# An encoder layer on one core: raw tiles of two gate/up jobs in query slots, a row norm behind a product, the last products in program order, and w_down raws on GpSimd's queue

## The chip, the cores and the metric

The kernel runs on one core of one Trainium2 chip. The metric is the device time of one execution in microseconds (us); lower is better. The times of before are the median of three runs and their extremes. One further execution was recorded by the hardware profiler, and every row below is of that one. Engines are named as in the profile: PE (TensorE's matmuls), DVE (VectorE), ACT (ScalarE), POOL (GpSimd), SP (SyncE, which here only issues DMAs).

## What is computed

One layer of a bidirectional encoder over two sequences of 512 tokens, width 1024, all in float32:

```
u = rms_norm(h, ln1);  z = u @ w_in            # pool_in 512 | c_q 384 | c_kv 256 | k_rope 32
y_pool = (window means of pool_in - pool_in) @ w_pool * pool_scale
q  = rms_norm(c_q)  @ w_qb;  k, v = rms_norm(c_kv) @ w_kvb   # 8 heads, rope, norms of q and k
h += concat(y_pool, softmax(q k^T) v) @ w_o
u2 = rms_norm(h, ln2);  h += (silu(u2 @ w_gate) * (u2 @ w_up)) @ w_down   # w_gate, w_up 1024 x 2816
out = h + sigmoid(rms_norm(h, ple_norm) @ w_ple_gate) * (p @ w_ple_proj)
```

## The kernel before

Activations lie with features on the 128 partitions and the 512 tokens of a sequence along the row, so a matmul writes a 128x512 PSUM bank. Every operand is held as a high and a low part, and one product of two 128-blocks is three matmuls (`mm3`, lines L157, L158, L159: high·high, then the two mixed ones). ACT makes the high part (L130), DVE or POOL the low part by a subtraction (`split`, L132 and L133).

The order of each engine's instructions is made by a scheduler from the program as it is written, and each engine then works its list strictly in order. Tiles come from tags with a fixed number of slots; a new tile of a tag waits until the readers of the tile that held its slot are done. So an edit to a tag or to the program's order moves rows on several engines.

The stages, in order of time. `latents()` (5 to 77 us) multiplies x by w_cq and w_ckv (`product`), and between them makes the row norm of x: `norm_columns` sums squares and takes the root on POOL, `norm_rows` makes `diag` on DVE (L203), multiplies it with ones on PE (L205, tile `rb`) and copies the result out on ACT (L209). `latent_norm` then squares c_q and c_kv on ACT (L330, tile `junk`). Pooling, projections and attention follow, then `output` (w_o).

The gate, up, down and gated-embedding products are Strassen-like. For a pair of weight blocks, `seven` runs seven products of n·3 matmuls each, named by the activation piece they take: B11, B21, T1, T2, T4, T3, B22. The activation pieces are sums and differences of normed halves: `normed_first` makes tiles x0 of sequence 0 (tag QK, 8 slots; the B21 pieces lie in the other four), `normed_rest` the norms of sequence 1 (L734) and the differences for T1 (L633), T2 (L763) and T4 (L766, the last readers of x0). The T4 pieces take the slots of x0 afterwards. The weight combinations are made by a generator, `stationary`: it loads two raw blocks (`load`, L143) and yields seven operand tiles from sums s (L648) and splits w (L130, L133). Operands are made up to eight ahead of the products (`fill`), in the order of the list `jobs`.

The first four gate/up jobs are cut in two: their part 0 gives only B11 and B21, part 1 the other five, so that part 1 loads the raws once more (tag R, 2 slots, on SP's queue). The hidden pieces made from gate and up are written to DRAM (`spill`, on SP's queue, tiles `st`, tensors op...) and read back by POOL's queue (`loaded`, tiles u, 512 KB each) for the w_down products; the saved h comes back the same way (`h_again`). w_down is worked in groups of (2, 3, 3, 3) blocks of rows; the 8 raw tiles of its first group (128x512, 256 KB) lie in tag F. The kernel ends with the gated embedding: `finish` applies the sigmoid, multiplies by the embedding (L986), adds h (L987) and stores.

Of the kernel before, what the change touches and what calls it, by code (L numbers as in the profile page):

```python
# [1 line left out]

# [1 line left out]

# [13 lines left out]
P = 128  # L18
# [11 lines left out]
QK = NOPE + ROPE  # L30
# [3 lines left out]
CKR = KVL + ROPE  # L34
# [54 lines left out]
def hybrid_layer(ctx: ExitStack, tc: tile.TileContext, a: dict, out: bass.AP):  # L89
    nc = tc.nc  # L90
# [9 lines left out]
    def sbuf(s, tag, shape, dt):  # L100
        return pool.tile([P] + shape, dt, tag=tag, name=nm(s), bufs=BUFS[tag])
# [4 lines left out]
    def Ft(s):  # L106
        return sbuf(s, "F", [T], F32)
# [10 lines left out]
    def Ps(s, tag=None):  # L118
        if tag is None:
            tag = ALL_BANKS[turn[0] * 3 % 8]  # L120
            turn[0] += 1
        return psum.tile([P, T], F32, tag=tag, name=nm(s), bufs=PSUM_BUFS[tag])

    def col(s, n=16, bufs=8):
        return pool.tile([P, n], F32, tag=f"c{n}", name=nm(s), bufs=bufs)

    def split(hi, lo, src, hi_eng="act", lo_eng=nc.vector):

        if hi_eng == "act":
            nc.scalar.activation(hi, src, AF.Copy)  # L130
        else:
            nc.vector.tensor_copy(hi, src)  # L132
        lo_eng.tensor_tensor(lo, src, hi.bitcast(F32), op=ALU.subtract)  # L133
# [6 lines left out]

    def load(src, n=D, tag="R"):
        raw = sbuf("raw", tag, [T if tag == "F" else D], F32)
        nc.sync.dma_start(raw[:, :n], src)  # L143
        return raw

    def weight(src, n=D, tag="W", hi="act", lo=None, raw_tag="R"):
# [8 lines left out]
    def mm3(ps, lhs, rhs, first, last, more=False):  # L155

        nc.tensor.matmul(ps, lhs[0], rhs[0], start=first, stop=False, skip_group_check=more)  # L157
        nc.tensor.matmul(ps, lhs[0], rhs[1], start=False, stop=False, skip_group_check=more)  # L158
        nc.tensor.matmul(ps, lhs[1], rhs[0], start=False, stop=last, skip_group_check=more)  # L159

    def act(t, sl=slice(0, T), rows=P):
        return t[:rows, 0, sl], t[:rows, 1, sl]

    def cols(w, i, n=P):
        return w[0][:, i:i + n], w[1][:, i:i + n]

    def tok(t):
        return slice(t * P, (t + 1) * P)
# [16 lines left out]
    def rsqrt(base, n, name):  # L185
        r = col(name)
        nc.gpsimd.tensor_tensor(r[:, :n], base, neghalf[:, :n], op=ALU.pow)
        return r

    def norm_columns(sq):  # L190

        ps = Ps("st", "g")
        for t in range(NT):
            nc.tensor.matmul(ps[:, t:t + 1], sq[:, tok(t)], ones[:, 0:1], start=True, stop=True)
        base = col("base")
        nc.vector.tensor_scalar(base[:, :NT], ps[:, :NT], 1.0 / D, EPS, op0=ALU.mult, op1=ALU.add)
        return rsqrt(base[:, :NT], NT, "r")

    def norm_rows(r, copy=True):

        diag = Ft("diag")
        for t in range(NT):
            nc.vector.tensor_scalar(diag[:, tok(t)], ident, r[:, t:t + 1], None, op0=ALU.mult)  # L203
        ps = Ps("rb", "g")
        nc.tensor.matmul(ps, ones, diag, start=True, stop=True)  # L205
        if not copy:
            return ps
        rb = Ft("rb")
        nc.scalar.activation(rb, ps, AF.Copy)  # L209
        return rb  # L210
# [31 lines left out]
    seqs = [Seq(), Seq()]  # L242
# [6 lines left out]
    def gained(q, k, x):  # L249
        g = At("gx", "A" if q is s0 else "QK")  # L250
        split_scaled(g, x, gcol(G_LN1 + k))
        q.gx.append(g)

    def latents():

        w_cq = []
        for q in seqs:
            q.gx, q.x = [], []
        for k2 in range(KD // 2):
            ws = a["w_cq"][:, k2 * 2 * QL:(k2 + 1) * 2 * QL]  # L260
            xs = [sbuf("x", "V" if q is s0 else "PT", [2, T], F32) for q in seqs]
            if k2 == 0:
                raw = sbuf("raw", "R", [D], F32)
                w = [sbuf("wh", "W", [D], F32R), sbuf("wl", "W", [D], F32R)]
                for i in range(2):
                    sl = slice(i * QL, (i + 1) * QL)
                    nc.sync.dma_start(xs[0][:, i, :], a["xT"][0, :, i, :])
                    if i == 0:
                        nc.sync.dma_start(gain, a["gains"])
                    nc.sync.dma_start(raw[:, sl], ws[:, sl])  # L270
                    split(w[0][:, sl], w[1][:, sl], raw[:, sl], "dve")
                    gained(s0, i, xs[0][:, i, :])
                w_cq.append(w)
            for q in seqs:
                if q is s1 or k2:
                    nc.sync.dma_start(xs[q.s], a["xT"][q.s, :, 2 * k2:2 * k2 + 2, :])
                    for i in range(2):
                        gained(q, 2 * k2 + i, xs[q.s][:, i, :])
                q.x += [xs[q.s][:, 0, :], xs[q.s][:, 1, :]]
            if k2:  # L280
                w_cq.append(weight(ws, 2 * QL, lo=eng("raw0", k2 == 3)))
            else:
                tables()
                nc.vector.tensor_scalar(gain[:QK, G_KN:G_KN + 1], gain[:QK, G_KN:G_KN + 1], float(QK) ** 0.5, None,
                                        op0=ALU.mult)

        def product(n, src, per, name, ws=None):
            acc = {(q, t): Ps(name, ALL_BANKS[q.s * NT + t]) for q in seqs for t in range(NT)}
            for k0 in range(0, KD, per):
                m = min(per, KD - k0)  # L290
                w = ws[k0 // per] if ws else weight(src[:, k0 * n:(k0 + m) * n], m * n)
                for q in seqs:
                    for k in range(k0, k0 + m):
                        for t in range(NT):
                            mm3(acc[q, t][:, :n], act(q.gx[k], tok(t)), cols(w, (k - k0) * n, n),
                                k == 0, k == KD - 1)
            res = {}
            for q in seqs:
                c = [sbuf(name, "A", [2, T], F32) for _ in range(NT // 2)]
                res[q] = [c[t // 2][:, t % 2, :] for t in range(NT)]  # L300
                for t in range(NT):
                    if t % 2:
                        nc.vector.tensor_copy(res[q][t][:, :n], acc[q, t][:, :n])
                    else:
                        nc.scalar.activation(res[q][t][:, :n], acc[q, t][:, :n], AF.Copy)
            return res

        cq = product(QL, a["w_cq"], 2, "cq", w_cq)
        for q in seqs:
            q.cq = cq[q]  # L310
            q.sq = Ft("sqx")
            for k in range(KD):
                square_sum(q.sq, q.x[k], k == 0, eng("sqx", k))
        for q in seqs:
            q.r1 = norm_columns(q.sq)
            q.rb = norm_rows(q.r1)
        ck = product(CKR, a["w_ckv"], 3, "ck")
        for q in seqs:
            latent_norm(q, q.cq, QL)
        for q in seqs:  # L320
            q.ck = ck[q]
            latent_norm(q, q.ck, KVL)
            rope_key(q)
# [345 lines left out]

    AHEAD = BUFS["W"]  # L670
    made, jobs = [], []

    def operands():
        while jobs:
# [11 lines left out]
    def seven(u, n, got, a_tag=None, tags=(None,)):  # L686


        def product(ps, b, first):
            w = made.pop(0)  # L690
            for j in range(n):
                mm3(ps, (w[:, 0, j * P:(j + 1) * P], w[:, 1, j * P:(j + 1) * P]), act(b[j]), first and j == 0, j == n - 1,
                    not first)
            fill()
            return ps

        def bank(name):
            t = tags[turn[0] % len(tags)]
            if t is not None:
                turn[0] += 1  # L700
            return Ps(name, t)

        a = product(Ps("a", a_tag), u["B11"], True)
        got(0, a)
        got(1, product(bank("c"), u["B21"], True))
        yield
        b = product(bank("b"), u["T1"], True)
        got(2, b)
        got(3, product(a, u["T2"], False))
        got(4, product(bank("d"), u["T4"], True))  # L710
        got(5, product(a, u["T3"], False))
        got(6, product(b, u["B22"], False))
# [29 lines left out]
    HALF = KD // 2  # L742
# [80 lines left out]
    last = output(s1, "V", None)  # L823
# [6 lines left out]
    PRO = len(HB)  # L830
    gu = [[a[w][f + i] for i in range(2)] for f in range(0, NF, 2) for w in ("w_gate", "w_up")]
    pg = [[a["w_pg"][m + i] for i in range(2)] for m in range(0, KD, 2)]
    jobs += [(w, HALF, 0) for w in gu[:PRO]] + [(w, HALF, 1) for w in gu[:PRO]] + [(w, HALF, None) for w in gu[PRO:]]
    f0 = 0
    for n in DOWN:
        f1 = f0 + 2 * n
# [256 lines left out]
```

## Time and profile before

| | |
|---|---|
| median of 3 runs | 1185.09 us |
| lowest, highest | 1184.77, 1187.89 us |
| profiled execution, own time | 1185.47 us |
| its span in the trace | 1183.7 us |
| its mean granted TensorE clock | 0.985 |
| PE busy | 1139.0 us, 96% |
| DVE busy | 896.1 us, 76% |
| ACT busy | 584.7 us, 49% |
| POOL busy | 229.7 us, 19% |

The own time is what the execution took on the device; the span is the part between the first and the last record, so 1.8 us lie around it. In a row of the timeline, the first number is the start in us from the span's start, the second the duration; "x8" joins neighbouring instructions of one kind; the bracket at the end is the engine's idle time before the row and what released it. In `out<-in`, the buffer numbers are left out. A granted clock of 1.00 is 2.4 GHz, of 0.5 is 1.2 GHz; a window's number is the mean over it.

### The profile page before, as it was taken

How to read it: one execution, taken by the hardware profiler on the slowest of the kernel's cores; microseconds unless marked ns; L12 is line 12 of the kernel's file. 1: busy time of each engine (PE TensorE's matmuls, PEld its weight loads, DVE VectorE, ACT ScalarE, POOL GpSimd, SP SyncE). 2: the span in 40 equal slices, each digit the busy share in tenths (PEclk: the TensorE clock that was granted, in tenths of full speed). 3: DMA queues.
4: the chain of work that ended last, by engine and by line, in shares of the span. 5: the costliest groups of instructions: out<-in, count | busy, mean ns of one | idle time of the engine just before them, and what ended most of it. 6: DMA issues, size and time to landing. Idle time of an engine off the chain costs nothing.

```text
span 1183.7 us, 14978 instructions
## 1 busy us (share of the span) xinstructions
PE 1139.0 (96%) x5168; PEld 923.7 (78%) x5168; DVE 896.1 (76%) x1639; ACT 584.7 (49%) x1135; POOL 229.7 (19%) x290
## 2 busy tenths in 40 slices
PE   8999989998999989999999999999999999999997
PEld 8898756775778867888888888888778888887775
DVE  7367867869584689987768776787597867885997
ACT  7144477878563445644445454554322222344643
POOL 3534364737110120000000000000322112001200
PEclk9899999998999998999999999999989999999999
DMA  6211100102233431554254433544998485636045
GB/s 219 70 54 47 51 0 1 54 19 72 89 116 116 142 107 35 203 190 165 94 187 168 170 118 131 181 175 156 407 413 328 159 323 186 220 91 224 27 162 185
DMA packets 53645, 173.25 MB, mean 146 GB/s; under 512 B 6209, under 2 KB 6977, under 8 KB 53569
## 3 DMA queue, kind: packets, MB, share of 16 engines
q1 hardware_dynamic: 41328, 127.73, 31.9%
q0 software_dynamic: 12240, 44.57, 9.7%
q8 instruction: 40, 0.66, 0.2%
q14 instruction: 37, 0.30, 0.1%
HBM read 119.33 MB, written 52.95 MB: 146 GB/s over the span
## 4 chain that ended last, share of the span: by engine, by line
PE 81%; DVE 9%; POOL 3%; issue 3%; DMA 2%; ACT 1%; SPq 0%; DVEq 0%; ACTq 0%; POOLq 0%
PE a L158 8%; PE a L157 8%; PE a L159 8%; PE b L157 6%; PE b L158 5%; PE b L159 5%; PE s L523 3%; PE d L158 3%; PE d L159 3%; PE d L157 3%; PE o L157 2%; PE o L158 2%; PE o L159 2%; PE c L157 2%; PE c L158 2%
## 5 line engine op out<-in xcount | busy, mean ns | idle before, releaser
L130 ACT ACTIVATE w<-s 128x512 fp32r<-128x512 f32 (+2 forms) x168 | 96.9, 579 | 159.0 <-DVE s L648 55.1
L157 PE MATMUL a<-u,w 128*128 128x512 f32 x444 | 171.6, 391 | 2.5 <-DVE h L949 1.9
L158 PE MATMUL a<-u,w 128*128 128x512 f32 x444 | 173.7, 391 | 0.2 <-POOL u L133 0.2
L159 PE MATMUL a<-u,w 128*128 128x512 f32 x444 | 171.1, 390 | 0.0
L130 ACT ACTIVATE w<-raw 128x512 fp32r<-128x512 f32 (+2 forms) x126 | 71.0, 577 | 138.4 <-PE a L159 83.9
L158 PE MATMUL b<-u,w 128*128 128x512 f32 x296 | 116.7, 395 | 4.1 <-DVE u L133 4.1
L133 DVE TENSOR_TENSOR w<-s,w 128x512 fp32r<-128x512 f32 (+2 forms) x168 | 103.9, 622 | 21.8 <-ACT w L130 21.2
L157 PE MATMUL b<-u,w 128*128 128x512 f32 x296 | 116.7, 395 | 2.9 <-ACT w L130 2.1
L159 PE MATMUL b<-u,w 128*128 128x512 f32 x296 | 116.0, 393 | 0.0
L157 PEld LDWEIGHTS a<-u,w 128*128 128x128 f32 x444 | 83.6, 189 | 21.6 <-DVE h L949 2.3
L158 PEld LDWEIGHTS a<-u,w 128*128 128x128 f32 x444 | 83.8, 189 | 17.9 <-POOL u L133 0.6
L159 PEld LDWEIGHTS a<-u,w 128*128 128x128 f32 x444 | 83.5, 188 | 17.4
L133 DVE TENSOR_TENSOR w<-raw,w 128x512 fp32r<-128x512 f32 (+2 forms) x126 | 78.5, 636 | 21.2 <-ACT w L130 21.2
L928 POOL DMA_DIRECT2D u<-opT4p x11 | 6.2, 565 | 402.0 <-DVE s L648 363.9
L158 PEld LDWEIGHTS b<-u,w 128*128 128x128 f32 x296 | 56.3, 190 | 16.9 <-DVE u L133 5.4
L157 PEld LDWEIGHTS b<-u,w 128*128 128x128 f32 x296 | 56.1, 190 | 16.8 <-ACT w L130 2.9
L523 PE MATMUL s<-qkT 96*128 96x512 f32 x128 | 65.1, 609 | 3.9 <-ACT p L527 3.2
L159 PEld LDWEIGHTS b<-u,w 128*128 128x128 f32 x296 | 56.4, 191 | 11.9
L157 PE MATMUL c<-u,w 128*128 128x512 f32 x148 | 58.6, 399 | 5.2 <-DVE x L734 5.2
L550 PE MATMUL y<-pt,v 128*128 128x512 f32 x128 | 59.3, 497 | 4.2 <-DVE pt L133 3.8
L158 PE MATMUL c<-u,w 128*128 128x512 f32 x148 | 58.5, 395 | 0.0
L159 PE MATMUL c<-u,w 128*128 128x512 f32 x148 | 58.4, 395 | 0.0
(238 smaller groups left out, 2760.1 us busy)
## 6 DMA issues: line engine op xcount, KB each, us to landing
raw<-in_w_gate SPq DMA_DIRECT2D x24, 512.0 KB, 4.0
raw<-in_w_up SPq DMA_DIRECT2D x24, 512.0 KB, 3.6
raw<-in_w_down SPq DMA_DIRECT2D x24, 384.0 KB, 3.4
raw<-in_w_o SPq DMA_DIRECT2D x16, 512.0 KB, 3.6
raw<-in_w_pg SPq DMA_DIRECT2D x12, 512.0 KB, 3.9
opB11p<-st SPq DMA_DIRECT2D x11, 512.0 KB, 2.6
opB21p<-st SPq DMA_DIRECT2D x11, 512.0 KB, 3.8
opT1p<-st SPq DMA_DIRECT2D x11, 512.0 KB, 4.4
```

Of the source, the lines that this page charges most:

```text
L130: nc.scalar.activation(hi, src, AF.Copy)
L133: lo_eng.tensor_tensor(lo, src, hi.bitcast(F32), op=ALU.subtract)
L157: nc.tensor.matmul(ps, lhs[0], rhs[0], start=first, stop=False, skip_group_check=more)
L158: nc.tensor.matmul(ps, lhs[0], rhs[1], start=False, stop=False, skip_group_check=more)
L159: nc.tensor.matmul(ps, lhs[1], rhs[0], start=False, stop=last, skip_group_check=more)
L523: nc.tensor.matmul(ps, qT[:, tok(t)], kT, start=True, stop=True)
L550: nc.tensor.matmul(q.y[h], vv, q.pt[h][j][:, i, :], start=(j == 0 and i == 0), stop=(j == NT - 1 and i == 1))
L928: nc.gpsimd.dma_start(d.bitcast(F32), spilled[k][f0 // 2 + j])
```

## The change

Four edits. First, raws of tag F (the first w_down group's eight) are loaded by GpSimd's DMA queue instead of SP's. Second, in `latents` the `norm_rows` of both sequences stands behind the product with w_ckv instead of ahead of it. Third, the very last product of the stream is issued behind the one before it, and does not get ahead of it. Fourth, the part 1 raws of the first two gate/up jobs (gate and up of the first pair of blocks) take slots of tag QK, where x0 lies, instead of slots of tag R.

```diff
     def load(src, n=D, tag="R"):
         raw = sbuf("raw", tag, [T if tag == "F" else D], F32)
-        nc.sync.dma_start(raw[:, :n], src)
+        (nc.gpsimd if tag == "F" else nc.sync).dma_start(raw[:, :n], src)
         return raw
...
         for q in seqs:
             q.r1 = norm_columns(q.sq)
+        ck = product(CKR, a["w_ckv"], 3, "ck")
+        for q in seqs:
             q.rb = norm_rows(q.r1)
-        ck = product(CKR, a["w_ckv"], 3, "ck")
         for q in seqs:
             latent_norm(q, q.cq, QL)
...
+    ended = []
...
         def product(ps, b, first):
             w = made.pop(0)
-            for j in range(n):
-                mm3(...)
+            with tc.issue_after(ended[0]) if not jobs and not made and ended else nullcontext():
+                for j in range(n):
+                    mm = mm3(...)
+            ended[:] = [mm.ins]
             fill()
             return ps
...
-    jobs += [(w, HALF, 0) for w in gu[:PRO]] + [(w, HALF, 1) for w in gu[:PRO]] + [(w, HALF, None) for w in gu[PRO:]]
+    jobs += [(w, HALF, 0) for w in gu[:PRO]] + [(w, HALF, 1, "QK") for w in gu[:2]] + [(w, HALF, 1) for w in gu[2:PRO]]
+    jobs += [(w, HALF, None) for w in gu[PRO:]]
```

What the edits do to the engines' lists is shown at three places. The names carry a running number behind the last underscore that is the same in both kernels. The line numbers of the changed kernel are up to five higher.

**The gate/up raws.** SP's list at the start of part 1, in before: raw956 and raw957 (w_gate), raw975 and raw976 (w_up) are the raws of the first two jobs, raw1025 and raw1026 those of the third.

```order
L143 DMA raw956_4300<-in_w_gate 128x1024
L891 DMA hsave1p3_4286<-h930_4088 128x1024
L143 DMA raw957_4302<-in_w_gate 128x1024
L143 DMA raw975_4400<-in_w_up 128x1024
L143 DMA raw976_4402<-in_w_up 128x1024
L143 DMA raw1025_4604<-in_w_gate 128x1024
L143 DMA raw1026_4606<-in_w_gate 128x1024
L853 DMA opB11p0_4202<-st1037_4674 128x1024
L143 DMA raw1042_4710<-in_w_up 128x1024
```

The same place in the changed kernel.

```order
L143 DMA raw1025_4604<-in_w_gate 128x1024
L896 DMA hsave1p3_4286<-h930_4088 128x1024
L143 DMA raw1026_4606<-in_w_gate 128x1024
L143 DMA raw956_4300<-in_w_gate 128x1024
L143 DMA raw957_4302<-in_w_gate 128x1024
L143 DMA raw975_4400<-in_w_up 128x1024
L143 DMA raw976_4402<-in_w_up 128x1024
L858 DMA opB11p0_4202<-st1037_4674 128x1024
L143 DMA raw1042_4710<-in_w_up 128x1024
```

The third job's w_gate raws have moved ahead, and the four raws of the first two jobs behind them; the slots that these four wait for now are those of x0910 to x0913. DVE's list in the changed kernel where those slots come free (td989 to td995 on L770 are the T4 differences that read x0 last, s and w the operands of the first job):

```order
L770 TENSOR_TENSOR td991_4460<-x0911_4012,td991_4460 128x512
L133 TENSOR_TENSOR u1006_4513<-x1985_4447,u1006_4513 128x512
L133 TENSOR_TENSOR u1008_4518<-x1986_4448,u1008_4518 128x512
L770 TENSOR_TENSOR td993_4465<-x0912_4013,td993_4465 128x512
L133 TENSOR_TENSOR u1010_4523<-x1987_4449,u1010_4523 128x512
L133 TENSOR_TENSOR u1012_4528<-x1988_4450,u1012_4528 128x512
L770 TENSOR_TENSOR td995_4470<-x0913_4014,td995_4470 128x512
L649 TENSOR_TENSOR s958_4304<-raw957_4302 128x512
L649 TENSOR_TENSOR s962_4324<-s958_4304,raw956_4300 128x512
L649 TENSOR_TENSOR s968_4361<-raw956_4300,raw957_4302 128x512
L133 TENSOR_TENSOR w959_4306<-s958_4304,w959_4306 128x512
L649 TENSOR_TENSOR s971_4380<-raw956_4300,s962_4324 128x512
```

In before the rows from s958 to s971 and nine more of these two jobs stand ahead of the norms of sequence 1, or between them and the T2 differences:

```order
L648 TENSOR_TENSOR s958_4304<-raw957_4302 128x512
L648 TENSOR_TENSOR s962_4324<-s958_4304,raw956_4300 128x512
L648 TENSOR_TENSOR s968_4361<-raw956_4300,raw957_4302 128x512
L133 TENSOR_TENSOR w959_4306<-s958_4304,w959_4306 128x512
L648 TENSOR_TENSOR s971_4380<-raw956_4300,s962_4324 128x512
L196 TENSOR_SCALAR base951_4191<-st950_4186 128x4
L133 TENSOR_TENSOR w963_4326<-s962_4324,w963_4326 128x512
L133 TENSOR_TENSOR w965_4343<-raw957_4302,w965_4343 128x512
```

They have moved behind the last T4 difference.

**The w_down raws.** GpSimd's list in before, at the loads of the second group (u1651 to u1656 are pieces read back from DRAM); no raw stands in this list.

```order
L928 DMA u1652_8198<-opT1p3_4227 128x1024
L928 DMA u1653_8199<-opT1p4_4228 128x1024
L928 DMA u1654_8203<-opT2p2_4237 128x1024
L928 DMA u1655_8204<-opT2p3_4238 128x1024
L928 DMA u1656_8205<-opT2p4_4239 128x1024
```

In the changed kernel the last five of the eight raws stand in the middle of these loads.

```order
L933 DMA u1652_8198<-opT1p3_4227 128x1024
L933 DMA u1653_8199<-opT1p4_4228 128x1024
L933 DMA u1654_8203<-opT2p2_4237 128x1024
L143 DMA raw1580_7855<-in_w_down 128x512
L143 DMA raw1592_7918<-in_w_down 128x512
L143 DMA raw1597_7942<-in_w_down 128x512
L143 DMA raw1609_8005<-in_w_down 128x512
L143 DMA raw1614_8029<-in_w_down 128x512
L933 DMA u1655_8204<-opT2p3_4238 128x1024
L933 DMA u1656_8205<-opT2p4_4239 128x1024
```

The fourth raw, raw1580, now stands behind the saved h tiles and ten loads of the second group. In before it was row 191 of SP's list, two rows behind the hidden piece opB11p10.

**The latent norm.** ACT's list in before: rb71 and rb77 are the copies of the row norm, junk the squares of c_q.

```order
L130 ACTIVATE wh155_864<-raw154_862 128x1024
L209 ACTIVATE rb71_452<-rb70_450 128x512
L209 ACTIVATE rb77_470<-rb76_468 128x512
L330 ACTIVATE junk100_703,ssq99_702<-cq46_378 128x384
L330 ACTIVATE junk101_705,ssq99_702<-cq46_378 128x384
L330 ACTIVATE junk102_707,ssq99_702<-cq47_379 128x384
```

In the changed kernel the same work is placed like this (wh147 to wh154 are weights of the pooling products, ck the copies of the w_ckv product).

```order
L305 ACTIVATE ck90_673<-ck74_456 128x288
L305 ACTIVATE ck91_678<-ck76_458 128x288
L305 ACTIVATE ck92_679<-ck78_460 128x288
L130 ACTIVATE wh195_1053<-raw194_1051 128x384
L209 ACTIVATE rb95_691<-rb94_689 128x512
L209 ACTIVATE rb98_700<-rb97_698 128x512
L331 ACTIVATE junk100_703,ssq99_702<-cq46_378 128x384
L331 ACTIVATE junk101_705,ssq99_702<-cq46_378 128x384
L331 ACTIVATE junk102_707,ssq99_702<-cq47_379 128x384
```

The two copies and all squares have moved behind the copies of the w_ckv product.

## Rows read from the trace of the kernel before

**Rows 1.** The page: busy time of each engine, and the chain that ended last, by engine.

```profile
PE 1139.0 (96%) x5168; PEld 923.7 (78%) x5168; DVE 896.1 (76%) x1639; ACT 584.7 (49%) x1135; POOL 229.7 (19%) x290
...
PE 81%; DVE 9%; POOL 3%; issue 3%; DMA 2%; ACT 1%; SPq 0%; DVEq 0%; ACTq 0%; POOLq 0%
```

**Rows 2.** Windows: each engine's busy time, granted TensorE clock, DMA share, GB/s.

```profile
40.00:75.00 35.00, 32.45 (x213) 30.70 (x212) 10.25 (x36) 11.50 (x34) 10.78 (x8) 0.90 0.18 51
400.00:475.00 75.00, 67.74 (x279) 54.13 (x279) 64.98 (x107) 36.97 (x65) 14.29 (x10) 0.93 0.26 85
475.00:500.00 25.00, 25.00 (x112) 20.66 (x111) 24.83 (x43) 15.65 (x30) 0.00 (x0) 1.00 0.58 204
...
850.00:875.00 25.00, 21.30 (x79) 16.45 (x79) 22.71 (x45) 7.40 (x19) 7.37 (x14) 0.86 1.03 412
```

**Rows 3.** Waits of PE, whole span: total, times, longest.

```profile
PE c L157 <- DVE x L734: 5.2, 1, 5.2
PE b L158 <- DVE u L133: 4.1, 3, 2.0
...
PE b L157 <- ACT w L130: 2.1, 2, 1.8
PE a L157 <- DVE h L949: 1.9, 1, 1.9
```

**Rows 4.** Timeline of PE, 46 to 80 us: start, duration, idle before.

```profile
52.75 2.08 PE L205 MATMUL rb<-diag,ones 128*128 128x512 f32 x2 [2.55 <-DVE diag L203]
```

**Rows 5.** The line of the latent norm's squares, on ACT.

```profile
L330 ACT ACTIVATE junk<-cq x8: 512/513/515, 64.1 to 67.7; 128x384 f32<-128x384 f32 x8
```

**Rows 6.** Timeline, 432 to 446 us, PE and DVE.

```profile
433.20 1.02 PE L205 MATMUL rb<-diag,ones 128*128 128x512 f32 x2
...
435.51 0.69 DVE L648 TENSOR_TENSOR s<-raw 128x512 f32<-128x512 f32 x1 [2.00 <-DMA raw<-in_w_up]
...
438.05 5.35 DVE L734 SCALAR_TENSOR_TENSOR x<-h,gain,rb 128x512 f32<-128x512 f32 x8
...
443.54 0.77 PE L157 MATMUL c<-u,w 128*128 128x512 f32 x1 [5.20 <-DVE x L734]
```

**Rows 7.** Timeline of DVE, 446 to 476 us.

```profile
458.36 0.68 DVE L766 TENSOR_TENSOR td<-x,td 128x512 f32<-128x512 f32 x1
...
463.18 0.68 DVE L766 TENSOR_TENSOR td<-x,td 128x512 f32<-128x512 f32 x1
463.78 3.69 DVE L133 TENSOR_TENSOR u<-td,u 128x512 fp32r<-128x512 f32 x6
```

**Rows 8.** Line L143 (raw loads), 422 to 464 us.

```profile
DMA to landing us min/median/max: 3.5/3.7/4.2
```

**Rows 9.** Timeline of GpSimd's queue, 838 to 882 us.

```profile
840.15 0.54 POOL L928 DMA_DIRECT2D u<-opB22p  x1 [0.74 <-PE a L159]
...
854.94 0.54 POOL L903 DMA_DIRECT2D h<-hsave0p  x1 [0.58 <-DMA u<-opB22p]
...
875.79 0.54 POOL L928 DMA_DIRECT2D u<-opT2p  x1 [0.67 <-issue]
```

**Rows 10.** Timeline of SP's queue, 838 to 882 us.

```profile
839.86 5.01 SPq L143 DMA_DIRECT2D raw<-in_w_down  x3
```

**Rows 11.** DMA, 820 to 890 us: the total, and one issue: count, KB, median us to landing.

```profile
DMA packets 8309, 27.98 MB, mean 400 GB/s; under 512 B 923, under 2 KB 923, under 8 KB 8303
...
raw<-in_w_down SPq DMA_DIRECT2D x8, 256.0 KB, 9.2
```

**Rows 12.** Timeline, 864 to 872 us, DVE and PE.

```profile
867.05 0.42 DVE L648 TENSOR_TENSOR s<-raw 128x256 f32<-128x256 f32 x1
...
868.03 0.63 PE L157 MATMUL b<-u,w 128*128 128x512 f32 x1 [1.80 <-ACT w L130]
```

**Rows 13.** Timeline of the end, 1172 to 1184 us.

```profile
1175.72 1.28 DVE L724 TENSOR_TENSOR x<-x,a 128x512 f32<-128x512 f32 x2 [2.03 <-PE a L159]
...
1179.34 1.28 DVE L987 TENSOR_TENSOR x<-x,h 128x512 f32<-128x512 f32 x2
```

More of the change, by code (lines that the diff above doesn't have):

```diff
@@ L1 @@
-from contextlib import ExitStack
+from contextlib import ExitStack, nullcontext
 import numpy as np
@@ L158, in mm3 @@
         nc.tensor.matmul(ps, lhs[0], rhs[1], start=False, stop=False, skip_group_check=more)
-        nc.tensor.matmul(ps, lhs[1], rhs[0], start=False, stop=last, skip_group_check=more)
+        return nc.tensor.matmul(ps, lhs[1], rhs[0], start=False, stop=last, skip_group_check=more)
     def act(t, sl=slice(0, T), rows=P):
@@ L690, in product @@
             w = made.pop(0)
-            for j in range(n):
-                mm3(ps, (w[:, 0, j * P:(j + 1) * P], w[:, 1, j * P:(j + 1) * P]), act(b[j]), first and j == 0, j == n - 1,
-                    not first)
+            with tc.issue_after(ended[0]) if not jobs and not made and ended else nullcontext():
+                for j in range(n):
+                    mm = mm3(ps, (w[:, 0, j * P:(j + 1) * P], w[:, 1, j * P:(j + 1) * P]), act(b[j]), first and j == 0,
+                             j == n - 1, not first)
+            ended[:] = [mm.ins]
             fill()
```

## The prediction

> **What bounds the kernel now.** I read the page first: PE is busy for 1139.0 of 1183.7 us, and the chain that ended last is 81% PE [rows 1]. So time can come only from places where PE stands still or runs at the lower clock, and can go wherever a new wait reaches PE. The windows show which stretches have slack: at 475 to 500 us PE has no idle time and a granted clock of 1.00, while 40 to 75, 400 to 475 and 850 to 875 us show idle time and 0.90, 0.93 and 0.86 [rows 2]. A delay ahead of a full stretch is not made good in it. The waits of PE name what ended last: the norms of sequence 1 (5.2 us, once), the pieces u (longest 2.0), a w_down operand (1.8) and the evacuation of a bank in w_down (1.9) [rows 3]. The edits touch all of these, and the end. I take them in order of time.
>
> **The norm behind w_ckv.** PE waits 2.55 us for the broadcast of the row norm in the middle of the w_ckv product [rows 4]. The lower clock that follows costs (1 − 0.90) × 35 = 3.5 us more, read from the window [rows 2]; both together are 6.05 us, and they vanish, since PE now goes through the product without the broadcast. But the copies of the broadcast, and all squares of the latents behind them, stand behind more of ACT's list. They began at 64.1 us [rows 5]. In the changed list the second broadcast stands behind all of w_ckv and 40 pooling products: about 69.4 + 40 × 0.227 + 1, some 80 us. So latent norms come 16 us later, and the pooling products that need ACT's and DVE's turn there wait instead of w_ckv. No row prices these waits. The bounds are −6.05 (all hidden under pooling) and +2 (all given back, and one more clock loss). By placing the later rows by hand at the durations of before, I find waits of about 1.2, 0.4 and 2.4 us on PE in pooling, and an attention that starts 1 us earlier. I take **−1.0**.
>
> **Raws in query slots.** The four raws wait for the T4 differences, the last readers of x0, and every operand of part 1 waits for the raws. In before, PE's row norm of sequence 1 stands at 433.20, DVE waits 2.00 for a w_up raw and works on operands, and the eight norms run from 438.05 to 443.40; PE resumes at 443.54 [rows 6]. In the changed list the norms have only that row norm ahead of them, and four matmuls fewer ahead of it: 433.20 − 0.9 + 1.02 makes about 433.4. Then come 8 norms (5.35) and 28 rows up to the last T4 difference, at 0.605 each (six rows take 3.69 with the last one's tail) [rows 7]: 433.4 + 5.35 + 16.9 = 455.7. In before it ended at 463.9 [rows 7], so DVE is ahead, but the operands are now behind it. The second raw is free six rows earlier, 452.1, and a raw takes 3.5 to 4.2 us to land [rows 8]: 456.1. The first sum (0.7) and its high part on ACT (0.6) make 457.5, so PE starts T1 at about 457.7. PE's last work is the up product's B21, ready at about 439 and done at 441.6: PE stands for 16 us where it stood 5.2.
>
> Against before: from 443.54 it had these 12 and 96 more matmuls, 108 × 0.227 = 24.5, a wait of 2.0 [rows 3], and (1 − 0.93) × 75 = 5.2 us of lower clock [rows 2], so it was through at 475.2. Now it is 457.7 + 96 × 0.227 + half of one 3.4 us stretch at the lower clock: 481.2. The difference is 6.0; placing the rows singly gives 6.6. I take **+6.5**. Bounds: +5 (the raw lands in 3.5 and the clock holds) and +9 (4.2, two stretches at the lower clock, and DVE behind PE for another us). DVE's wait for the w_up raw is gone, but nothing is waiting for it any more.
>
> **w_down raws on GpSimd's queue.** SP issued the third, fourth and fifth raw at 839.86 to 844.87 [rows 10]. On GpSimd's list the fourth is behind eight h tiles and ten u tiles. That queue is far behind its place in the program: the u load issued at 840.15 was waited for by the h load at 854.94, eight loads later, and the tenth u load of the next group was issued only at 875.79 [rows 9]. The transfers are the bound here: 400 GB/s mean over 820 to 890 us [rows 11], DMA share 1.03 [rows 2], so 512 KB cost 1.31 us and 256 KB 0.66.
>
> From the landing of that u load there are 1 u, 8 h and 10 u ahead of the fourth raw, 19 × 1.31 = 24.9, then the third and the fourth raw, 1.3. SP's hidden pieces share the engines: four that were issued by 858 and two that have moved ahead of the fourth raw's first sum on DVE, 6 × 1.31 = 7.9. The start is 854.94, or 853.0, since three raws are no longer in front of it on SP's queue. So the fourth raw lands between 853.0 + 26.2 = 879.2 (no share for SP) and 854.94 + 34.1 = 889.0. I take 885.5, near to where the spills have been served. In before its first sum ran at 867.05 and PE took the operand at 868.03 [rows 12]; the same 0.98 makes 886.5, or 18.5 us later. PE's list around this product has nothing to put before it: 8 matmuls of the third raw's block, then it stands. The stretch behind is full, so it is not made up. For DVE's two rows less behind it I take half a us off: **+18.0**, bounds +11 and +22. The stall of 1.8 and the clock loss that before has at the same place [rows 3, 12] are in both.
>
> Here a rule of the Trainium skill speaks against me: "Trainium Kernel Development and Optimization", Key Constraints, says that DMAs issued from SP, ACT and GpSimd run on the same 16 DMA engines and interleave, so that issuing from several only saves issue time. By that alone this edit would cost nothing, and the sum would be 1189.5. The rows show waits inside one queue's list, which the rule doesn't speak of.
>
> **Last products in program order.** In before the final T3 product's two chains start when PE ends: the additions at 1175.72, the last addition of h ends at 1180.62 [rows 13], 4.9 us. In the changed list T3 ends 12 × 0.227 = 2.7 us ahead of B22, and only one chain (addition, sigmoid, product, addition: about 0.6 + 0.65 + 0.65 + 0.7, plus 0.6 for DVE being at another chain) is behind the last matmul: 3.4. So **−1.5**, bounds 0 (the stores' landing is the end anyway) and −2.2.
>
> **Sum.** 1185.47 − 1.0 + 6.5 + 18.0 − 1.5 = 1207.5 us, against the profiled execution's own time, which is 0.4 above the median of the runs. What a measurement here can tell from no change is 0.3%, 3.6 us.
>
> **Rivals.**
> *Queue without price.* The raws land as before: 1207.5 − 18.0 = 1189.5, just slower. For it: the same transfers share the same bandwidth on either queue. Against it: loads in one list are issued in order, and rows 9 show 15 us from an issue to the use of its landing. 0.10. The rule quoted above gives this case.
> *Part 1 hidden.* PE finds the T1 operands on time because the raws wait for less than I read: −6.5, 1201.0. For it: DVE is 8 us ahead there. Against it: PE has only 12 matmuls left. 0.10.
> *GpSimd's queue runs ahead.* With five raws off it, SP's queue gives GpSimd's loads the bandwidth, and the fourth raw lands before 867.05, which is the point that decides. Then the operand wait of 1.8 and the bank wait of 1.9 [rows 3] go too, with the clock loss of (1 − 0.86) × 25 = 3.5: 1189.5 − 7.2 = 1182.3, within the margin, and not slower; with all 6.05 of the first edit kept it is 1177.3, faster. Against it: 26 us of transfers from 853 stand ahead of the raw. 0.08, 0.03 of it faster.
> *All waits fall short.* Both large terms are wrong for a reason that I don't see: about 1183, 0.05.
>
> **How the numbers follow.** The forecast's case has 0.67, by its own bounds 1198 to 1213. The range, 1189 to 1213, takes in the first two rivals and leaves out the tails and the last two. Faster: 0.06 (0.03 from the third rival, 0.03 from the last). Same: 0.08 (0.05, 0.02 and a little of the first). Slower: 0.86.
>
> **What would show it.** In the changed trace: no wait for the diagonal at 52 us and no lower clock behind it, squares of c_q from about 80 us; a PE wait of about 16 us for an operand of the first gate job, with raws issued only after the T4 differences; a PE wait of 14 to 20 us for a w_down operand in the first group, with GpSimd's raws issued behind ten u loads; the last addition some 3.4 us behind the last matmul. I am wrong if the two long waits aren't there: if the raws are issued before the T4 differences, or if the fourth w_down raw lands by the time PE comes to its product.

## The result, and the profile after

| | before | after |
|---|---|---|
| median, us | 1185.12 (4 runs) | 1218.09 (4 runs) |
| lowest, highest | 1184.77, 1187.89 | 1217.38, 1220.26 |
| ratio, 95% interval | | 1.0281 (1.0264 to 1.0297) |
| span of the profiled execution | 1183.7 | 1218.5 |

The change costs 33 us. The forecast was 1207.5, with a range up to 1213: the direction was right, the size was not, and the result lies outside the range. The profiled execution of the changed kernel is the slowest of its four (1220.26 us).

The page of the changed kernel, busy time of each engine and the chain that ended last, answers to [rows 1]:

```profile
PE 1144.2 (94%) x5168; PEld 924.2 (76%) x5168; DVE 894.9 (73%) x1639; ACT 587.7 (48%) x1135; POOL 233.0 (19%) x298
...
PE 81%; DVE 10%; ACT 3%; issue 3%; DMA 2%; POOL 1%; SPq 0%; DVEq 0%; ACTq 0%; POOLq 0%
```

The work is the same (PE has 5168 matmuls in both), and the span is 34.8 us longer: it is waiting time. The waits of PE in the changed kernel (total, times, longest) answer to [rows 3]:

```profile
PE b L157 <- ACT w L130: 31.3, 3, 16.3
...
PE yp L157 <- ACT devT L130: 4.8, 1, 4.8
...
PE kv L157 <- DVE v L133: 3.2, 1, 3.2
```

Two waits for a weight operand hold almost all of the 31.3; they are the two that the prediction named. The waits for devT and v are in pooling and the projections. In before no wait for v is over 0.3 us, and the wait for devT is this one:

```profile
PE yp L157 <- ACT devT L130: 1.4, 1, 1.4
```

The windows of the changed kernel (PE, PEld, DVE, ACT, POOL busy, then granted clock, DMA share, GB/s) answer to [rows 2]:

```profile
40.00:75.00 35.00, 35.00 (x247) 33.84 (x245) 7.91 (x33) 6.86 (x12) 12.44 (x8) 1.00 0.25 78
75.00:160.00 85.00, 74.40 (x331) 60.77 (x330) 62.42 (x182) 39.64 (x106) 33.05 (x24) 0.94 0.13 39
...
450.00:475.00 25.00, 8.35 (x25) 6.33 (x26) 23.87 (x41) 12.11 (x21) 0.00 (x0) 0.67 0.24 84
875.00:900.00 25.00, 10.52 (x32) 7.11 (x30) 11.60 (x20) 2.77 (x6) 7.59 (x14) 0.70 1.03 416
```

The window from 75 to 160 us of the kernel before, which was not shown ahead of the prediction:

```profile
75.00:160.00 85.00, 82.87 (x405) 69.57 (x405) 66.14 (x186) 41.15 (x98) 34.94 (x25) 1.00 0.16 48
```

From 40 to 75 us the changed kernel has won what it should: PE is busy throughout and at full clock. From 75 to 160 us it loses 8.5 us of busy PE and, at a clock of 0.94, 5.1 us more. That is the stretch that the prediction priced too low. Net of the 6 us that are won up to 75 us, 8.9 us are lost by the 800th matmul (161 us in before). The rest of the 11.3 below comes by the 1000th (208 us), where four runs without this edit lose about 1.5 us against the same trace too.

To see how much each stage adds, the start of the n-th matmul is compared in the two traces, at places where both have done the same work. The times are counted from the first matmul, which starts 0.2 us later in the changed kernel. The differences, after minus before:

| done by | matmuls | after − before, us | added in the stage | predicted |
|---|---|---|---|---|
| the first gate/up products | 2000 | +11.3 | +11.3 (second edit) | −1.0 |
| all of part 1's start | 2160 | +19.4 | +8.1 (fourth) | +6.5 |
| the first w_down group | 3920 | +36.5 | +17.1 (first) | +18.0 |
| the last matmul | 5168 | +36.3 | −0.2 | 0 |
| the end of the span | | +34.6 | −1.7 (third) | −1.5 |

From 2080 to 3700 matmuls and from 3920 on, the difference stays where it is to 0.4 us: here a delay ahead of a full PE is not made good.

**The fourth edit's stage.** Timeline of the changed kernel, 436 to 475 us: SP's queue, DVE and PE, the rows that answer to [rows 6 to 8]; the last line is the wait of SP's queue for the T4 differences, 400 to 480 us (total, times, longest).

```profile
443.83 1.02 PE L205 MATMUL rb<-diag,ones 128*128 128x512 f32 x2
...
462.35 1.53 SPq L143 DMA_DIRECT2D raw<-in_w_gate  x2
465.36 2.13 SPq L143 DMA_DIRECT2D raw<-in_w_up  x2
...
461.59 0.69 DVE L770 TENSOR_TENSOR td<-x,td 128x512 f32<-128x512 f32 x1
...
468.18 0.69 DVE L649 TENSOR_TENSOR s<-raw 128x512 f32<-128x512 f32 x1 [1.09 <-DMA raw<-in_w_gate]
...
469.65 0.80 PE L157 MATMUL b<-u,w 128*128 128x512 f32 x1 [16.26 <-ACT w L130]
...
SPq L143 <- DVE td L770: 31.1, 4, 27.5
```

The first raw is issued at 462.35, when the first T4 difference has ended (461.59 + 0.69), and PE stands for 16.26 us until the first operand that comes from this pair. The prediction had 16.

**The first edit's stage.** Timeline of the changed kernel, 860 to 912 us: GpSimd's queue, DVE and PE, the rows that answer to [rows 9, 12].

```profile
871.72 0.55 POOL L143 DMA_DIRECT2D raw<-in_w_down  x1 [0.74 <-DVE w L133]
...
881.69 0.54 POOL L933 DMA_DIRECT2D u<-opB11p  x1 [0.68 <-DMA raw<-in_w_down]
...
891.25 0.54 POOL L933 DMA_DIRECT2D u<-opT2p  x1 [0.75 <-DVE td L883]
892.53 0.56 POOL L143 DMA_DIRECT2D raw<-in_w_down  x1 [0.74 <-DMA u<-opB21p]
...
902.99 0.42 DVE L649 TENSOR_TENSOR s<-raw 128x256 f32<-128x256 f32 x1 [10.31 <-DMA raw<-in_w_down]
...
903.98 0.80 PE L157 MATMUL b<-u,w 128*128 128x512 f32 x1 [14.79 <-ACT w L130]
```

The third raw goes out at 871.72, the fourth at 892.53, right behind the tenth u load at 891.25; it has landed 10.5 us later, when DVE begins its first sum. PE takes the operand 0.99 us after that sum begins, as in before (0.98). The landing of the third raw releases the load at 881.69, which is seven places behind it, and every load of this list from 856 to 904 us goes out 0.3 us after the landing of the one seven places ahead. The list keeps seven loads on their way, so the fourth raw can go out only when the ten loads ahead of it have gone out at the pace of the landings.

**The end.** Timeline of the changed kernel, the last rows of PE and DVE; they answer to [rows 13].

```profile
1211.72 0.39 PE L159 MATMUL b<-u,w 128*128 128x512 f32 x1
...
1212.68 0.68 DVE L728 TENSOR_TENSOR x<-x,b 128x512 f32<-128x512 f32 x1
...
1214.79 0.69 DVE L992 TENSOR_TENSOR x<-x,h 128x512 f32<-128x512 f32 x1
```

The last addition ends at 1215.48, 3.5 us after the last matmul is done (1211.72 + 0.23). In before the last matmul starts at 1175.24 and the last addition ends at 1180.62, so the same stretch was 5.2 us. (The 4.9 us of the prediction are counted from the first of the last additions.)

### The profile page after: what moved, and what is told of

Its sections match the earlier page's. It is cut to its first block, busy times and chain, and to the rows that moved or that the text cites. A ratio compares the mean times of both kernels' runs of the same rounds, so it can differ in the third digit from the quotient of the medians.

```text
span 1218.5 us, 14971 instructions
## 1 busy us (share of the span) xinstructions
PE 1144.2 (94%) x5168; PEld 924.2 (76%) x5168; DVE 894.9 (73%) x1639; ACT 587.7 (48%) x1135; POOL 233.0 (19%) x298
## 4 chain that ended last, share of the span: by engine, by line
PE 81%; DVE 10%; ACT 3%; issue 3%; DMA 2%; POOL 1%; SPq 0%; DVEq 0%; ACTq 0%; POOLq 0%
PE a L158 8%; PE a L159 8%; PE a L157 8%; PE b L157 5%; PE b L158 5%; PE b L159 5%; PE s L524 4%; PE d L158 3%; PE d L157 3%; PE d L159 3%; PE o L157 2%; PE c L159 2%; PE o L159 2%; PE c L157 2%; PE o L158 2%
## 5 line engine op out<-in xcount | busy, mean ns | idle before, releaser
L157 PE MATMUL b<-u,w 128*128 128x512 f32 x296 | 117.6, 398 | 33.1 <-ACT w L130 31.3
L524 PE MATMUL s<-qkT 96*128 96x512 f32 x128 | 67.9, 631 | 3.5 <-ACT p L528 3.4
L130 ACT ACTIVATE wh<-raw 128x1024 fp32r<-128x1024 f32 (+4 forms) x37 | 35.6, 965 | 58.0 <-PE o L158 21.9
L158 PE MATMUL d<-u,w 128*128 128x512 f32 x148 | 57.9, 391 | 0.6 <-DVE u L133 0.6
L157 PE MATMUL c<-u,w 128*128 128x512 f32 x148 | 57.6, 392 | 0.5 <-DVE x L738 0.5
```

What stands on the lines that cost most here:

```text
L524: nc.tensor.matmul(ps, qT[:, tok(t)], kT, start=True, stop=True)
```

## The experiments

The theory after the result: three edits cost by themselves (the norm 11.3, the raws' slots 8.1, the queue 17.1 us), and the prices add up; the third edit wins 1.7. In the changed kernel's first part, ACT's squares of the latents run like this (line, count, duration, first and last start):

```profile
L331 ACT ACTIVATE junk<-cq x8: 509/510/514, 82.1 to 86.6; 128x384 f32<-128x384 f32 x8
```

They began at 64.1 in before [rows 5], so they are 18 us late. Each experiment's difference is taken to the kernel before on the same chip, whose median moved between 1183.9 and 1184.3 there; the changed kernel itself was not run again there. The ratio is not the quotient of the two medians; in the first three rows the two differ by about 0.2%, 2 to 3 us.

| run | what differs | median | to before, us | ratio, 95% interval |
|---|---|---|---|---|
| u1_norm_ahead | changed, second edit undone | 1207.22 | +23.2 | 1.0218 (1.0192 to 1.0243) |
| u2_raws_in_R | changed, fourth edit undone | 1211.18 | +27.2 | 1.0249 (1.0227 to 1.0271) |
| u3_raws_on_SP | changed, first edit undone | 1199.95 | +16.0 | 1.0157 (1.0130 to 1.0184) |
| u4_end_only | before, third edit alone | 1182.81 | −1.2 | 0.9996 (0.9981 to 1.0011) |
| a1_norm_behind | before, second edit alone | 1195.03 | +10.8 | 1.0080 (1.0050 to 1.0110) |
| a2_norm_behind_swapped | a1, sequence 1's norm first | 1197.08 | +12.8 | 1.0099 (1.0065 to 1.0133) |
| m1_bcast_behind_ckv | before, broadcasts right behind w_ckv | 1188.10 | +4.2 | 1.0039 (1.0022 to 1.0056) |
| m2_loads_behind_raws | before, first edit, loads behind raws | 1188.25 | +4.4 | 1.0031 (1.0015 to 1.0048) |
| m3_raws_in_A | before, raws in tag A | 1183.20 | −0.7 | 0.9986 (0.9969 to 1.0003) |
| f1_A_raws_and_end | m3 and third edit | 1182.61 | −1.6 | 0.9976 (0.9956 to 0.9996) |

### Each edit undone, or alone

The first three runs take one edit of the changed kernel back (the reverse of its hunk in the diff above); the fourth is the kernel before with only the hunk in `seven`.

> The changed kernel with the row norm back ahead of the w_ckv product; the other three edits stay. Theory: the edits' prices add up, and the norm's is what the changed trace shows by the attention's end, 11.3 us. So 1218.1 - 11.3 = 1206.8 (1205 to 1208.5). Rival: the delay in pooling only moves waits that would come later anyway, and part of it comes back: under 6 us, 1212 or more. The prediction's own price, 1 us gained, would give 1219.

> The changed kernel with the four gate/up raws back in tag R. Theory: their wait for the T4 differences costs 8.1 us (19.4 - 11.3 at equal numbers of matmuls), so 1218.1 - 8.1 = 1210.0 (1208.5 to 1211.5), and PE waits 5 us for the norms there again. Rival: the stall there is only a shift of the delay that pooling brings, and undoing it gives under 4 us: 1214 or more.

> The changed kernel with the w_down raws back on SP's queue. Theory: their place behind ten loads costs 17.1 us (36.5 - 19.4 at equal numbers of matmuls): 1218.1 - 17.1 = 1201.0 (1199.5 to 1202.5), no wait of PE over 3 us in the first w_down group. Rival: the transfers as a whole are late there, on either queue, and the undoing gives under 8 us: 1210 or more.

> The kernel before with the third edit alone, the very last product issued behind the one before it. Theory: -1.7 us (the end of the changed kernel lies 34.8 later where its last matmuls lie 36.3 to 36.5 later): 1183.4 (1182.8 to 1184.2). Rival: the end is set by the landing of the stores, and nothing changes: 1185.1.

Undoing the norm leaves +23.2 of the changed kernel's +33.0, so by the medians it is worth 9.8; undoing the raws' slots 5.8; undoing the queue 17.0. Together with the −1.2 of the third edit these make 31.4 of 33.0. By the ratios the three are smaller (7.5, 3.8 and 14.7, each uncertain by 3 to 4 us), so the times alone would not prove the sum. The traces do, since a stage adds about the same whatever the other edits are. What each stage adds at equal numbers of matmuls, each run's trace against that of before (the last row is the stretch itself):

| stage (matmuls) | runs with the edit | runs without it |
|---|---|---|
| norm (1 to 2000) | 11.3, 10.7, 11.3, 11.8, 11.4 | −0.8 to +0.8 in five |
| raws' slots (2000 to 2160) | 8.1, 7.3, 6.3 | −1.3 to −0.2 in six, raws in tag R |
| queue (2160 to 3920) | 17.1, 16.9, 16.2 | −2.0 to +0.3 in seven |
| end (last matmul to the span's end) | 6.8 in six | 8.5 in six |

The column on the right also says how far two traces of the same work differ: by 1 to 2 us in a stage. With the raws back in tag R, PE waits 5.0 us for the norms again. The third edit alone is not resolved by its timing (the interval holds 1), but its 1.7 us stand in every trace that has it.

### The norm: what makes it cost more than it wins

> The kernel before with the second edit alone. Theory: this edit by itself costs what it costs in the changed kernel: +11.3 us on the kernel before of the same chip (+9.5 to +13). Rival: part of it shows only with the other edits: under +7.

+10.8, as the theory has it. Two causes were open. In the changed trace DVE waits 9.7 us for the copy of the second broadcast (theory one), and ACT's squares start 18 us late (theory two). The next run takes the first away and keeps the second; its edit against the run before it:

```diff
         ck = product(CKR, a["w_ckv"], 3, "ck")
-        for q in seqs:
+        for q in reversed(seqs):
             q.rb = norm_rows(q.r1)
```

> As the run with the second edit alone, but the row norm of sequence 1 is made first. The first pooling product belongs to sequence 1, so that DVE's first pooling work needs the first broadcast (done at 75.7 in the changed trace) and not the second (82.1). ACT's squares of the latents stay behind both copies, at 82. Theory one, that DVE's wait of 9.7 us for the second broadcast is the price: 6.4 us of it go, +5 on the kernel before (+3 to +7). Theory two, that the squares on ACT and the latent norms behind them are the price, since DVE's pooling rows that PE needs stand behind these norms: only the two or three us of DVE work that can be done ahead are won, +8.5 (+7 to +11).

The waits of DVE from 55 to 165 us in the run with the second edit alone:

```profile
DVE u L399 <- ACT rb L209: 9.7, 1, 9.7
```

With sequence 1's norm first that row is gone; DVE waits for pooling products instead (10.4 us in three waits). The line of the squares in that run:

```profile
L331 ACT ACTIVATE junk<-cq x8: 508/509/514, 81.7 to 86.2; 128x384 f32<-128x384 f32 x8
```

And PE's longest wait from 60 to 165 us:

```profile
PE yp L157 <- ACT devT L130: 7.7, 1, 7.7
```

Theory one falls: the 9.7 us wait is gone, and the time is not better but 12.8 above before. The squares start at 81.7 as in the changed kernel, and PE's wait for devT has grown from 4.8 (in the run with the second edit alone too) to 7.7 us. devT is made from a difference (dev) that stands on DVE behind the latent norms, which stand behind the squares. Theory two also expected 2 or 3 us to be won; they were not, and the time lies above its range too. Another run, made before these two, brings the squares forward (the comments in its edit are not in the code).

```diff
         for q in seqs:
             q.r1 = norm_columns(q.sq)
-            q.rb = norm_rows(q.r1)
+            q.dg = norm_diag(q.r1)      # the four diag rows of norm_rows
         ck = product(CKR, a["w_ckv"], 3, "ck")
+        for q in seqs:
+            q.rb = norm_bcast(q.dg)     # its matmul and its copy
...
-    steps(pools, 1)
+    with tc.issue_after(behind[0]):     # the last broadcast's matmul
+        steps(pools, 1)
```

> The kernel before with one change: the diagonals are made ahead of the w_ckv product as before, the two broadcasts and their copies behind it, and the first pooling products are issued behind the broadcasts (in the changed kernel 40 pooling products stood ahead of the second one). Theory: what costs 11.3 us is that second broadcast, for which DVE waits 9.7 us and ACT's squares start 17.9 us later; right behind w_ckv it comes at about 71 instead of 81 us, and some 9 of the 11.3 are not lost: 1187 (1184 to 1190). Rival: the squares' place behind the copies of w_ckv is enough, as they still start 8 us later than in before: 1193 or more.

The squares of this run:

```profile
L347 ACT ACTIVATE junk<-cq x8: 514/515/516, 72.0 to 75.5; 128x384 f32<-128x384 f32 x8
```

They start 10 us earlier than in the changed kernel and 8 later than in before, and the price falls from 10.8 to 4.2 (3.5 at equal matmuls). PE's wait for devT is no longer among its waits there. The link between the squares and PE is the first row of dev on DVE; here it is in before, in this run, in the run with the second edit alone and in the swapped one (timelines of DVE, 60 to 108 us):

```profile
88.61 0.69 DVE L411 SCALAR_TENSOR_TENSOR dev<-win,u 128x512 f32<-128x512 f32 x1
...
93.18 0.68 DVE L428 SCALAR_TENSOR_TENSOR dev<-win,u 128x512 f32<-128x512 f32 x1
...
101.10 0.68 DVE L412 SCALAR_TENSOR_TENSOR dev<-win,u 128x512 f32<-128x512 f32 x1
...
102.24 0.68 DVE L412 SCALAR_TENSOR_TENSOR dev<-win,u 128x512 f32<-128x512 f32 x1
```

In the three runs it starts when the last row of the latent norms ends (93.3, 101.2 and 102.3). So the price follows this row: 4.6, 12.5 and 13.6 us late cost 4.2, 10.8 and 12.8. What PE wins in the w_ckv product is already taken off. A broadcast in the middle of the w_ckv product, which might keep the squares where they were and spare PE its wait, was not run.

### The w_down raws: the queue or the place in it

```diff
-        nc.sync.dma_start(raw[:, :n], src)
+        d = (nc.gpsimd if tag == "F" else nc.sync).dma_start(raw[:, :n], src)
+        if tag == "F":
+            fraw[:] = [d.ins]
...
-            with tc.issue_after(back.ins):
+            with tc.issue_after(fraw[0] if f0 == 2 * DOWN[0] else back.ins):
                 u = loaded(n, f0)
```

> The kernel before with the first edit alone, but the loads of the second w_down group stand behind the last of the eight raws on GpSimd's queue. Theory: the price is that of the ten loads ahead of the fourth raw; without them the raw comes when DVE is ready for it, and the 17.1 us are gone: 1185 (1183 to 1188). Rival: GpSimd's queue is too far behind for any raw (eight transfers in flight, 15 us from issue to landing), and the fourth raw is still some 8 us late: 1191 or more.

+4.4: of 17 us some 13 are gone, and the rival's 6 or more are not there, but the time is just above the theory's range, whose middle was nothing. PE's waits in this run, 830 to 910 us:

```profile
PE b L161 <- ACT w L130: 2.6, 1, 2.6
PE a L161 <- DVE h L953: 1.8, 1, 1.8
PE b L161 <- issue: 1.4, 1, 1.4
```

The long wait of 14.8 has become 2.6, against 1.8 in before [rows 3]. So the place behind ten loads made most of the price. A small one is left, 2.4 us at equal matmuls. Its cause is open: the first sum of the fourth raw waits only 0.24 us for that raw, and a list without the h tiles ahead of it was not run.

### The gate/up raws: whose slots

```diff
-    ... + [(w, HALF, 1) for w in gu[:PRO]] + ...
+    ... + [(w, HALF, 1, "A") for w in gu[:2]] + [(w, HALF, 1) for w in gu[2:PRO]] + ...
```

> The kernel before with the four gate/up raws in tag A (20 slots) instead of R or the query slots. There they are loaded ahead of the last w_o weights. Theory: the price of the fourth edit lies in who holds the slots, not in leaving tag R: with the raws there early, DVE's waits for them (3.1 and 2.0 us) are gone, the norms start some 4.6 us earlier, and PE's 5.2 us wait with part of the lower clock behind it goes: 1180 (1177 to 1183). Rival: the operands take DVE's time wherever the raws lie, and the third job's earlier raws push the norms back: 1185 or more.

The timing does not tell it from no change, and misses the expectation. Its stage did improve: at equal matmuls it goes from +0.8 to −2.7 over part 1's start. The runs with the raws in tag R lose 0.2 to 1.3 against the same trace there, so some 2 to 3 us of the 3.5 are the edit's. PE's waits there, 400 to 480 us:

```profile
PE b L158 <- DVE u L133: 3.3, 1, 3.3
PE b L157 <- ACT u L130: 1.3, 1, 1.3
PE c L157 <- DVE x L734: 1.0, 1, 1.0
```

The wait for the norms has gone from 5.2 to 1.0, as the theory says, and 2.6 us of it come back as waits for the pieces u, as the rival says: DVE has the same rows to do. That tag R is left is not what costs; the wait for slots that x0 holds is.

### A version that is ahead of both

> The kernel before with the four gate/up raws in tag A and the last product behind the one before it, and nothing else. Theory: the 3.5 us that the first gave in its stage and the 1.5 at the end add up: -4 on the kernel before (-2 to -5.5). Rival: as the raws' run alone timed only 0.7 below before, what it wins in its stage is within what one kernel's executions differ by: -1.5 or less.

1.6 us by the medians, 0.24% by the ratio, which is 2.8 us (interval 0.04% to 0.44%): ahead of the kernel before, if by little. The medians lie between the rival's figure and the theory's range, the ratio inside that range, so which of the two holds stays open.

## Why the prediction was wrong, point by point

**The norm behind w_ckv** is the step that failed: "No row prices these waits. The bounds are −6.05 (all hidden under pooling) and +2 (all given back, and one more clock loss)", with −1.0 taken. Measured: +11.3 in the changed kernel, +10.8 alone. The first half was right: no wait at 52 us, full clock from 40 to 75, and squares from 82.1 where 80 was forecast. The fault was to let the loss be no larger than the gain. A delay of 18 us at the head of a chain over ACT, DVE and PE isn't bounded by the 6 us that PE won by it; its bound is the 18 us, less the slack behind it. Of the 18 us 12.2 reach the first row of dev (100.83 in the changed kernel, 88.61 in before). The slack behind that row was to be read from before: PE is busy there for 82.87 of 85 us at full clock, and it already waits 1.4 us for devT, so that operand has none. The waits placed by hand in pooling (1.2, 0.4 and 2.4, together 4.0) are 0.5, 4.8 and 1.1 in the trace, together 6.4; those in the projections (3.2 and 0.7 for v, and two of 0.2) and the lower clock from 75 to 160 (5.1 us) were not seen at all. The gain, too, was read from one execution: five other runs that keep the norm ahead wait 2.5 to 2.8 us for its diagonal, but their granted clock from 40 to 75 us is 0.95 in four and 1.00 in one, where before has 0.90. With +11.3 in the place of −1.0 the sum is 1207.5 + 12.3 = 1219.8, against 1220.26 of the profiled execution.

**Raws in query slots**: +6.5 forecast, within +5 to +9; 6.3 to 8.1 in the traces, 5.8 by the undoing. The mechanism stands in the rows, to the 16 us wait of PE. The half stretch of lower clock behind the wait (1.7 us) had no row; in the changed trace 13 matmuls from 469.65 to 475.36 follow each other 0.43 us apart instead of 0.23, an estimated 2.7 us.

**w_down raws**: +18.0 forecast, within +11 to +22; 17.1 in the trace and 17.0 by the undoing. One reading was off: two u loads of one name went out at 840.15 and 841.43, and the h load at 854.94 waited for the second of them. The list keeps seven loads on their way and not eight, which moves the landing from which the term is counted by 1.4 us, within its bounds. The prediction weighed a rule of the Trainium skill against this term ("Trainium Kernel Development and Optimization", Key Constraints): DMAs issued from SP, ACT and GpSimd run on the same 16 engines, and issuing from several only saves issue time. The first half agrees with the traces, where the engines are as full as before (share 1.03 in both). Read as a forecast, the second half would give nothing for this edit, and the measurement decides against that: what stood ahead on GpSimd's list cost 17 us, and with the loads behind the raws most of it was gone.

**Last products**: −1.5 forecast; −1.7 in the traces, not resolved by the timing of the edit alone. The pieces that the prediction names add up to 3.2 and not to its 3.4, which would have made it −1.7.

**The range** failed for the first step's reason: with +11.3 for the norm and the other terms at their forecasts the sum is already above 1213. It was also narrower than its terms: their upper bounds (+2, +9, +22 and 0) add up to 1218.5, and the prediction does not say how that became 1213. That 1218.5 is close to the measured time is luck, as the norm's bound in it is wrong by 9 us.

## What to carry to other kernels

A row that moves later on an engine delays everything behind it in that engine's list, so in these runs the price of a move followed how late the moved chain became at its last row ahead of PE, and not the wait that the move removed; read the slack from the stage that follows: does PE already wait for an operand of that chain there? Before a load is given to another queue, or a tile to another tag, list what stands ahead of it there and who holds the slot: ten loads and one late reader cost 17 and 8 us here, and the same edits with the loads behind, or with free slots, cost 4 and nothing. Where PE was full behind the stage, no delay was made good. And a difference of two single traces is good to 1 or 2 us in a stage; count the same stage in runs that don't have the edit before a small gain is believed.

## What the runs showed of the hardware that was not expected

Some small DVE instructions last until a POOL subtraction beside them ends. Timeline of the changed kernel, 95 to 104 us, DVE and POOL:

```profile
96.71 1.90 DVE L337 TENSOR_TENSOR rl<-rl,r 128x4 f32<-128x4 f32 x1
...
98.64 1.23 DVE L351 TENSOR_SCALAR krsq<-krsq 128x4 f32<-128x4 f32 x1
...
96.24 2.36 POOL L133 TENSOR_TENSOR wl<-raw,wh 128x1024 fp32r<-128x1024 f32 x1
98.56 1.29 POOL L133 TENSOR_TENSOR wp<-raw,wp 128x512 fp32r<-128x512 f32 x1
```

Rows of four columns mostly take 0.15 to 0.17 us; these two end at 98.61 and 99.87, when POOL's two subtractions end (98.60 and 99.85). They lie in the chain of the latent norms, but they don't set the two kernels apart. In before three rows of that stretch are held up in the same way: 2.38 us at 69.48, 1.53 at 76.99 and 1.25 at 84.81, beside POOL subtractions of 2.55, 1.84 and 1.29. Beside a POOL row of L187 small DVE rows stay short: from 92.2 to 93.2 us in the changed kernel they take 0.15 to 0.18 us, beside one of 1.06.

The granted clock behind the same waits differs between executions. From 850 to 875 us PE waits 1.9 us for the evacuation of a bank and 1.8 for an operand in before, in m3_raws_in_A and in f1_A_raws_and_end; the window's granted clock is 0.86, 0.86 and 0.93. In u4_end_only, with these two waits and one of 0.9 more, it is 1.00:

```profile
850.00:875.00 25.00, 20.41 (x88) 15.81 (x87) 23.26 (x48) 7.63 (x19) 7.04 (x13) 1.00 1.03 413
```

So a loss of clock read from one window of one execution, as the prediction did three times, is not a fixed price.
